# One layer of an SSD and MLP hybrid on one core: the gate's row by a transposition and DRAM instead of TensorE, and three shifts in the SSD stage's plan

## The chip, the core and the metric

The kernel runs on one core of one Trainium2 chip. The metric is the device time of one execution in microseconds (us). Three runs of the kernel before took 967.64, 968.88 and 969.93; the median, 968.88, is the time before. One further execution was taken with a profile; every duration in this text comes from it.

## The reference

One layer of a trunk with two parallel head groups. There are 256 latent tokens (`x`), 256 context tokens (`ctx`), and a width of 2048:

```
shift, scale, gate = split(silu(c) @ w_ada + b_ada, 3)            # for x; the same with c_ctx for ctx
z   = (rmsnorm(x, g_pre) * (1 + scale) + shift) @ w_in            # ctx: only the columns of x, B, C and dt
xBC = silu(depthwise_conv(z[x, B, C], width 5))                   # rows of 64 latent tokens, one row of 256 for ctx
y   = SSD forward + SSD backward                                  # 8 groups of 4 heads, chunks of 128 tokens
      # per group: CB = C B^T; y_diag = (CB * exp(min of decays)) x; states = B^T (x * decay); y_off = C states
a   = rmsnorm((y + d_skip * x) * silu(z_ssd), g_ssd)
b   = rmsnorm(u * (w_s @ rmsnorm(v, g_v) + b_s) * silu(z_mlp), g_mlp)
out = rmsnorm(concat(a, b) @ w_out, g_post)
return x + gate * out                                             # gate: one number per channel, 2048 of them
```

The scan of the latent tokens starts from the states that the context leaves, in both directions. All data is fp32. The part of the change that bears on the last line is the product `gate * g_post`, a row of 2048 numbers that must stand on all 128 partitions (called `G`), since there the tokens lie on the partitions.

## The kernel before

**Products.** Each fp32 operand is split into a rounded part (`hi`) and the rest (`lo`), and each product is three matmuls on TensorE, hi by hi, lo by hi and hi by lo (`mm3`, L139 to L143). The weights come in halves of 128 x 1024, each of which takes a cast on ScalarE (L87, L543) and a subtraction on VectorE (L88, L549) and serves 24 matmuls of the projection; the splits run some halves ahead of TensorE.

**Stages.** From 0 to about 130 us the modulation, the norm and seven channel tiles of the projection; from 130 to 445 us the SSD stage; from 445 to about 800 us the latent stage with 16 blocks for v, u and the two gate paths (`pa`, L1219 to L1221); then the out projection (L1260 to L1262) and the final norm.

**The SSD stage.** The channels of x, B and C are cut into 32 tiles of 128, ordered by group: tile 4g and 4g+1 are x of group g, 4g+2 is B, 4g+3 is C. Seven of them (0 to 3, 12, 13 and 15) are made in the first stage; 12, 13 and 15 wait in SBUF (`zq`). The loop over `REST` (L1024) makes the other 25: 48 matmuls each into a PSUM tile `psx` of the pool `acp`, which has two banks, so a tile may start once the tile before the last has been read. A C tile is needed for the latent tokens alone and has 256 columns instead of 512. After the projection a tile goes through `conv_tile` (L595): tap 0 on ScalarE (L608), eight tap instructions on VectorE (L624, the last ones that read the bank), SiLU on ScalarE (L627).

**The order of the work.** The order on TensorE, VectorE, ScalarE and GpSimd is the order in which the program issues it; only the DMA queue of SyncE (SP) is ordered by the scheduler. Between the matmuls a small planner issues the rest: `later(dt, fn)` (L578) puts a step on a list, due `dt` units from now, and `pump` (L582) moves the planner's clock on by 1.3 units after every six matmuls of a full tile (0.65 in a C tile) and issues what is due. A unit is about a microsecond. `plan_tile` (L976) gives the steps of each tile their due times. When the C tile of group g is made, it plans for that group: the scores `pcb` (L852) and the states `psc` and `psl` (L869, L872) at 6 units plus `late`; masks `cbb` and `cbf` (L860), M on GpSimd (L897); the carried states `hs`; `M` and the decayed scores in `E` (L905, L907); `pso` (L921) and its decay `yo` on VectorE (L927); the `y` sums on GpSimd (L935); the product `psy` with x (L947); its transposition `yc` (L739, called from `ssd_yc`), which goes through DRAM. For the next group it plans the four additions to the row tile R on ScalarE (`ssd_d`, L821), the minimum of the two directions into E on VectorE (`ssd_min`, L828) and the exponential of E on ScalarE (`ssd_e`, L834).

**Transposed tiles.** x and B are needed with tokens on partitions. In groups 1 to 6 they are transposed in 32 by 32 blocks on VectorE (`turn`, L738), written to DRAM and read back in four pieces by SP's queue (`turned`, L745; `bk` for B at L747, `xk` for x), with 4.5 units reserved for this (`LAND`). In groups 0 and 7 TensorE does it. `xw` and `xl` (L786, L793, GpSimd) are x times decay, the other operand of the states.

**The row load.** R of the next group, 1 MB read from one DRAM row onto all partitions, is issued on GpSimd's queue by `row_load` (L721), from `ssd_min` (L830), once E of this group no longer needs the buffer; the buffer is the only one.

**The gate.** In the latent stage VectorE multiplies each of 16 row blocks of `w_ada` by silu(c) and sums (`gate_tile`, L1070), which leaves the gate as 128 x 16 numbers, channel on the partition. After block 9 `gate_bcast` (L1075) makes G from it: g_post is read onto all partitions into G; the gate is transposed by a matmul with the identity (`psgt`, L1095), split, spread by VectorE into a block pattern (`gd`), and four matmuls with ones (`pg`, L1105) give the gate on all partitions, which VectorE multiplies into G. In the blocks nearby, `lat_t` (L1116) transposes the gated latents through DMAs on GpSimd's queue (`vt`, L1124, 16 per block), and `lat_split` (L1127) splits them, with its cast `hhi` at L1140. G is read at the end, in `o_gate` (L1311).

Of the kernel before, what the change touches and what calls it, by code (L numbers as in the profile page):

```python
# [15 lines left out]
P = 128  # L16
D = 2048
# [16 lines left out]
LAST = (-1, 4, 5, 0, 1, 2, 3, 6)  # L34

WSSD = (0, 1, 2, 3, 4, 12, 5, 6, 13, 7, 8, 14, 9, 10, 15, 11)
C_BADA, C_GPRE, C_GSSD, C_GMLP, C_BS, C_CW, C_CB, NPC = 0, 48, 64, 80, 96, 112, 272, 304


def _tile_order():  # L40
# [7 lines left out]
def tile_hybrid_ssd_mlp(  # L48
# [7 lines left out]
    pcols: bass.AP,  # L56
    dtp: bass.AP,
    dskip: bass.AP,
    gpost: bass.AP,
    gv: bass.AP,  # L60
    wst: bass.AP,
    wxbc: bass.AP,
# [66 lines left out]
    bab = stp.tile([P, KT, 2], F32, name="bab")  # L129
    nc.vector.tensor_scalar(bab[:, :, 0], pc[:, C_BADA + 16 : C_BADA + 32], 1.0, None, op0=ALU.add)  # L130
    nc.vector.tensor_copy(bab[:, :, 1], pc[:, C_BADA : C_BADA + 16])
    gate = cpool.tile([P, 48], F32, name="gate")
    nc.gpsimd.memset(gate, 0.0)
    cpool.tile([P, 64], F32, name="cpad")

# [36 lines left out]
    def spt(shape, name):  # L172
        return sps.tile(shape, F32, tag="s", name=name)
# [650 lines left out]
    def ssd_min(g, c):  # L824
        R = rows_[g]
        if c == 0:
            gs_.setdefault(g, {})["E"] = cv1.tile([P, 2, 4, P], F32, tag="E", name=f"E{g}")
        nc.vector.tensor_tensor(gs_[g]["E"][:, c], R[:, :, 0, c, :], R[:, :, 1, c, :], op=ALU.min)  # L828
        if c == 1:
            row_load(g + 1)  # L830

    def ssd_e(g):
        E = gs_[g]["E"]
# [185 lines left out]
    plan_tile(3, psx[3], 29, ds=5, late=2)  # L1019
    plan_d(17, 0, 1.3)  # L1020
    plan_e(22.5, 0)
    plan_tile(12, zq[0], 70, ds=7, tx=9)
    plan_tile(13, zq[1], 80, ds=7, tx=12.5)
    for n, i in enumerate(REST):  # L1024
        lat = ORDER[i] >= 24
# [49 lines left out]
    def gate_bcast():  # L1075
        gs.close()
        gp = ctx.enter_context(mkpool(name="gp", bufs=1, side="right"))
        G = gp.tile([P, D], F32, name="G")
        L_["G"] = G
        nc.gpsimd.dma_start(G, gpost.partition_broadcast(P))  # L1080
        nc.vector.tensor_tensor(gate[:, 0:16], gate[:, 0:16], pc[:, C_BADA + 32 : C_BADA + 48], op=ALU.add)
        nc.vector.tensor_copy(gate[:, 32:48], gate[:, 0:16])


        gh = gp.tile([48, P], F32R, name="gh")
        gl = gp.tile([48, P], F32R, name="gl")
        g1 = gp.tile([48, P], F32R, name="g1")
        gd = gp.tile([48, 4, P], F32R, name="gd")
        gk = gp.tile([48, KT], F32, name="gk")
        nc.scalar.copy(g1, ones[0:48])  # L1090
        nc.vector.tensor_tensor(gk, ident[0:48, 0:16], ident[0:48, 32:48], op=ALU.add)

        def rows():
            ps = spt([48, P], "psgt")
            nc.tensor.matmul(ps, lhsT=gate, rhs=ident, start=True, stop=True)  # L1095
            nc.scalar.copy(gh, ps)
            nc.vector.tensor_tensor(gl, ps, gh.bitcast(F32), op=ALU.subtract)
            nc.vector.tensor_copy(gh[32:48], gl[32:48].bitcast(F32))

        def expand(j):  # L1100
            nc.vector.tensor_tensor(gd, bc(gh.bitcast(F32), 1, 4), bc(gk[:, 4 * j : 4 * j + 4], 2, P), op=ALU.mult)

        def spread(j):
            p = spt([P, 512], f"pg{j}")
            nc.tensor.matmul(p, lhsT=g1, rhs=gd, start=True, stop=True)  # L1105
            gb = G[:, j * 512 : (j + 1) * 512]
            nc.vector.tensor_tensor(gb, p, gb, op=ALU.mult)
            if j < 3:
                expand(j + 1)

        later(2, rows)
        later(4, lambda: expand(0))
        for j in range(4):
            later(7 + 3 * j, lambda j=j: spread(j))
# [253 lines left out]
    man.close()  # L1368


_INS = ["xch", "xtok", "ccols", "crow", "wada", "pcols", "dtp", "dskip", "gpost", "gv", "wst", "wxbc", "wlat", "wsp", "wout"]
_OUTS = [((256, 2048), "float32")]


def _layout(i):
    import numpy as np

    i = {k: np.asarray(v) for k, v in i.items()}
    x, c, cx = i["x"][0], i["c"][0], i["ctx"][0]
    w_in, w_out, w_ada = i["w_in"][0], i["w_out"][0], i["w_ada"][0]  # L1380
    order = _tile_order()
    a = {}
    xc = np.concatenate([cx, x], axis=0)
    a["xch"] = xc.T.reshape(4, 4, P, TOK).transpose(0, 2, 1, 3).reshape(4, P, D)
    a["xtok"] = x.reshape(2, P, D)
    a["ccols"] = np.stack([c.reshape(KT, P).T, i["c_ctx"].reshape(KT, P).T], axis=2)
    wada = np.empty((48, P, D), w_ada.dtype)
    ss = w_ada[:, : 2 * D].reshape(KT, P, 2, KT, 4, 32)[:, :, ::-1].transpose(0, 1, 4, 3, 2, 5)
    sd = w_ada[KD * P :, : 2 * D].reshape((KT - KD) * P, 2, KT, P)[:, ::-1].transpose(0, 2, 1, 3)
    for kt in range(NSING):  # L1390
        r = ss[:, :, :, kt] if kt == 0 else ss[:, :, :, kt].transpose(0, 1, 3, 2, 4)
        wada[2 * kt : 2 * kt + 2] = r.reshape(2, 8, P, 256).transpose(0, 2, 1, 3).reshape(2, P, D)
    for m in range(NSING, KT, 2):
        wada[2 * m] = sd[:, m : m + 2].transpose(3, 1, 2, 0).reshape(P, D)
        wada[2 * m + 1 : 2 * m + 4] = ss[:KD, :, :, m : m + 2].reshape(3, 4, P, 512).transpose(0, 2, 1, 3).reshape(3, P, D)
    wada[32:] = w_ada[:, 2 * D :].reshape(KT, P, 16, P).transpose(2, 3, 0, 1).reshape(16, P, D)
    a["wada"] = wada
    cw = i["conv_w"][0].reshape(5, 32, P)[:, order].transpose(2, 1, 0).reshape(P, 160)
    cb = i["conv_b"][0].reshape(32, P)[order].T
    a["pcols"] = np.concatenate(  # L1400
        [i["b_ada"][0].reshape(48, P).T, i["g_pre"][0].reshape(KT, P).T, i["g_ssd"][0].reshape(KT, P).T,
         i["g_mlp"][0].reshape(KT, P).T, i["b_s"][0].T, cw, cb], axis=1)
    a["dtp"] = np.stack([i["dt_bias"][0].reshape(64), i["a_log"][0].reshape(64)])
    a["dskip"] = i["d_skip"].reshape(1, 32)
    a["gpost"] = i["g_post"].reshape(1, D)
    a["gv"] = i["g_v"].reshape(1, D)
    a["crow"] = c.reshape(1, D)
    wk = w_in.reshape(KT, P, -1)
    xbc = wk[:, :, :4096].reshape(KT, P, 32, P)[:, :, order]
    a["wst"] = np.concatenate([wk[:, :, 4096:4160], xbc[:, :, list(FIRST)].reshape(KT, P, NST * P)], axis=2)  # L1410
    a["wxbc"] = xbc[:, :, list(REST)].transpose(2, 1, 0, 3).reshape(len(REST), P, D)
    cols = {"z": 4160, "u": 6208, "v": 8256, "m": 10304}
    blocks = []
    for n in "vumz":
        w = wk[:, :, cols[n] : cols[n] + 2048].reshape(4, 4, P, 4, 512)
# [28 lines left out]
```

## Time and profile before

| what | value |
|---|---|
| median of the runs | 968.88 us |
| profiled execution, its own time | 968.23 us |
| span of its profile | 966.5 us |
| TensorE clock granted | 1.00 |
| TensorE (PE) busy | 954.9 us |
| VectorE (DVE) busy | 686.7 us |
| ScalarE (ACT) busy | 482.2 us |
| GpSimd (POOL) busy | 192.5 us |
| moved by DMA | 224.57 MB |

The span runs from the first to the last instruction that the profile shows; the execution's own time is 1.7 us longer. A row of a timeline has its start, its busy time, engine, line, operation, output<-inputs and shape; `x4` says that four instructions in a row are drawn together, and square brackets hold the idle time before it and what ended that. A row of a waiting list names the engine and instruction that waited, what it waited for, and the total, the number of times and the longest. `SPq` and `POOLq` are DMA queues. A line that groups by stretch gives the window, its sum of busy time on TensorE and then each engine's busy time with its count, the granted clock, the DMA share and GB/s.

### The profile page before, as it was taken

What the parts mean: (1) busy time and instruction counts of PE and PEld (TensorE: products, weight loads), DVE (VectorE), ACT (ScalarE), POOL (GpSimd) and SP (SyncE); (2) the same over time, 40 slices, a digit from 0 to 9 for tenths busy, and PEclk for the clock granted to TensorE, in tenths of its full rate; (3) what the DMA queues carried; (4) which work ended last, traced back from release to release, by engine and by line L of the source; (5) the groups of instructions that cost most, each with busy time, mean ns of one, the idle gap of its engine ahead of it and who ended that gap; (6) DMA issues with size and microseconds to landing.
All of it is one profiled execution on the core that took longest, in us unless ns stands there. A gap on an engine that the chain in (4) does not pass through costs nothing.

```text
span 966.5 us, 13778 instructions
## 1 busy us (share of the span) xinstructions
PE 954.9 (99%) x5142; PEld 771.1 (80%) x5142; DVE 686.7 (71%) x1116; ACT 482.2 (50%) x732; POOL 192.5 (20%) x290
## 2 busy tenths in 40 slices
PE   9999999999999999999999999999999999999997
PEld 4688888777787878787888888887888888888885
DVE  6888798879887877866667687767666665445636
ACT  4344458554555544455445333455566564346512
POOL 0000002532533414323000000043335440000000
PEclk9999999999999999999999999999999999999999
DMA  9999965566659767647877767785666666556722
GB/s 367 416 416 415 371 228 166 145 187 156 136 151 229 170 179 163 164 143 248 317 295 281 285 259 273 285 302 197 198 226 214 215 214 216 198 181 255 261 87 87
DMA packets 141490, 224.57 MB, mean 232 GB/s; under 512 B 110816, under 2 KB 111072, under 8 KB 118768
## 3 DMA queue, kind: packets, MB, share of 16 engines
q1 hardware_dynamic: 134640, 206.03, 63.2%
q0 software_dynamic: 6208, 16.85, 5.6%
q8 instruction: 40, 0.66, 0.3%
q10 hardware_dynamic: 576, 0.82, 0.2%
q14 instruction: 26, 0.21, 0.1%
HBM read 210.76 MB, written 8.72 MB: 227 GB/s over the span
## 4 chain that ended last, share of the span: by engine, by line
PE 83%; DVE 7%; DMA 5%; issue 1%; SPq 1%; POOL 1%; ACT 1%; DVEq 0%; POOLq 0%; ACTq 0%
PE pa L1219 12%; PE pa L1220 12%; PE pa L1221 12%; PE psx L141 7%; PE psx L142 6%; PE psx L143 6%; PE pm L1260 3%; PE pm L1261 3%; PE pm L1262 3%; DMA ada<-in_wada_dram 3%; DVE xbc L624 3%; PE pq L1262 2%; PE pq L1260 2%; PE pq L1261 2%; PE psada L254 2%
## 5 line engine op out<-in xcount | busy, mean ns | idle before, releaser
L88 DVE TENSOR_TENSOR lo_w<-w,hi_w 128x1024 fp32r<-128x1024 f32 x173 | 210.5, 1222 | 138.1 <-ACT hi_w L87 137.9
L87 ACT CAST hi_w<-w 128x1024 fp32r<-128x1024 f32 x173 | 181.9, 1053 | 211.1 <-PE pa L1221 139.3
L1219 PE MATMUL pa<-hi_w,hhi 128*128 128x512 f32 x512 | 201.1, 393 | 0.0
L1221 PE MATMUL pa<-hi_w,hlo 128*128 128x512 f32 x512 | 199.3, 389 | 0.0
L1220 PE MATMUL pa<-lo_w,hhi 128*128 128x512 f32 x512 | 199.3, 389 | 0.0
L141 PE MATMUL psx<-hhi,hi_w 128*128 128x512 f32 (+1 forms) x400 | 151.5, 379 | 0.2 <-DVE xbc L624 0.2
L143 PE MATMUL psx<-hhi,lo_w 128*128 128x512 f32 (+1 forms) x400 | 145.7, 364 | 0.0
L142 PE MATMUL psx<-hlo,hi_w 128*128 128x512 f32 (+1 forms) x400 | 145.6, 364 | 0.0
L1219 PEld LDWEIGHTS pa<-hi_w,hhi 128*128 128x128 f32 x512 | 96.1, 188 | 21.2 <-issue 1.6
L1221 PEld LDWEIGHTS pa<-hi_w,hlo 128*128 128x128 f32 x512 | 96.1, 188 | 20.3
L1220 PEld LDWEIGHTS pa<-lo_w,hhi 128*128 128x128 f32 x512 | 96.1, 188 | 19.5 <-issue 0.2
L624 DVE SCALAR_TENSOR_TENSOR xbc<-psx,pc,xbc 128x248 f32<-128x248 f32 (+1 forms) x204 | 83.5, 473 | 26.0 <-ACT xbc L608 25.2
L549 DVE TENSOR_TENSOR lo_w<-w,hi_w 128x1024 fp32r<-128x1024 f32 x61 | 76.8, 1265 | 19.7 <-ACT hi_w L543 19.6
L141 PEld LDWEIGHTS psx<-hhi,hi_w 128*128 128x128 f32 x400 | 75.5, 189 | 14.8 <-issue 3.5
L142 PEld LDWEIGHTS psx<-hlo,hi_w 128*128 128x128 f32 x400 | 75.5, 189 | 12.9 <-issue 1.7
L143 PEld LDWEIGHTS psx<-hhi,lo_w 128*128 128x128 f32 x400 | 75.5, 189 | 12.3
L543 ACT CAST hi_w<-w 128x1024 fp32r<-128x1024 f32 x61 | 63.5, 1044 | 29.5 <-PE psx L142 16.6
L1260 PE MATMUL pm<-hi_w,hhi 128*128 128x512 f32 x128 | 49.8, 389 | 0.0
L1261 PE MATMUL pm<-lo_w,hhi 128*128 128x512 f32 x128 | 49.8, 389 | 0.0
L1262 PE MATMUL pm<-hi_w,hlo 128*128 128x512 f32 x128 | 49.8, 389 | 0.0
L1124 POOL DMA_DIRECT2D y<-T x64 | 36.8, 583 | 47.8 <-ACT sq L1195 33.1
L1124 POOL DMA_DIRECT2D vt<-T x64 | 36.8, 584 | 47.3 <-ACT sq L1195 34.8
(277 smaller groups left out, 1424.1 us busy)
## 6 DMA issues: line engine op xcount, KB each, us to landing
w<-in_wlat_dram SPq DMA_DIRECT2D x64, 1024.0 KB, 4.9
w<-in_wout_dram SPq DMA_DIRECT2D x32, 1024.0 KB, 4.8
w<-in_wxbc_dram SPq DMA_DIRECT2D x25, 1024.0 KB, 6.0
ada<-in_wada_dram SPq DMA_DIRECT2D x24, 1024.0 KB, 13.9
gate<-in_wada_dram SPq DMA_DIRECT2D x16, 1024.0 KB, 5.0
ada<-in_wada_dram SPq DMA_DIRECT2D x16, 512.0 KB, 12.4
R<-acs POOLq DMA_DIRECT2D x8, 1024.0 KB, 7.1
wst<-in_wst_dram SPq DMA_DIRECT2D x15, 480.0 KB, 13.0
```

The source lines that it names most:

```text
L87: nc.scalar.copy(hi, raw)
L88: nc.vector.tensor_tensor(lo, raw, hi.bitcast(F32), op=ALU.subtract)
L141: nc.tensor.matmul(ps, lhsT=whi, rhs=hhi[k][:, s], start=start, stop=False)
L142: nc.tensor.matmul(ps, lhsT=whi, rhs=hlo[k][:, s], start=False, stop=False)
L143: nc.tensor.matmul(ps, lhsT=wlo, rhs=hhi[k][:, s], start=False, stop=stop)
L624: nc.vector.scalar_tensor_tensor(ao, zi, cw[:, k : k + 1], ao, op0=ALU.mult, op1=ALU.add)
L1219: nc.tensor.matmul(pa[tk], lhsT=hhi[k][:, t], rhs=whi[:, w], start=k == 0, stop=False)
L1220: nc.tensor.matmul(pa[tk], lhsT=hhi[k][:, t], rhs=wlo[:, w], start=False, stop=False)
L1221: nc.tensor.matmul(pa[tk], lhsT=hlo[k][:, t], rhs=whi[:, w], start=False, stop=k == KT - 1)
L1260: nc.tensor.matmul(p, lhsT=yh[:, t], rhs=whi[:, w], start=j == 0, stop=False)
L1261: nc.tensor.matmul(p, lhsT=yh[:, t], rhs=wlo[:, w], start=False, stop=False)
L1262: nc.tensor.matmul(p, lhsT=yl[:, t], rhs=whi[:, w], start=False, stop=hf == 0 and j == 15)
```

## The change

**Gate's row.** g_post is no input of its own any more; it comes as 16 more columns of the table `pcols` (`C_GPOST`), channel on the partition like the gate. `gate_bcast` adds the bias and multiplies by g_post on VectorE (128 x 16), transposes the 128 x 32 tile in blocks of 32 on VectorE, writes the row to DRAM with four DMAs and reads it onto all partitions with one, all five on GpSimd's queue, right after block 9. The matmuls `psgt` and `pg`, their casts and their tiles are gone. Since one argument line is gone, a line such as L852 before is L851 after, up to this function.

**SSD: three numbers.** `late`, the delay of all steps of a group after its C tile, grows by 3 units where B goes through DRAM (groups 1 to 6): 11 becomes 14, and 14 becomes 17 in group 3. The row load of group 5 is issued 12 units after its minimum instead of at once. And tile 12, the first x tile of group 3 that waits in SBUF, is planned from 63 instead of 70.

```diff
-C_BADA, C_GPRE, C_GSSD, C_GMLP, C_BS, C_CW, C_CB, NPC = 0, 48, 64, 80, 96, 112, 272, 304
+C_BADA, C_GPRE, C_GSSD, C_GMLP, C_BS, C_CW, C_CB, C_GPOST, NPC = 0, 48, 64, 80, 96, 112, 272, 304, 320
...
-    gate = cpool.tile([P, 48], F32, name="gate")
+    gate = cpool.tile([P, 32], F32, name="gate")
...
         if c == 1:
-            row_load(g + 1)
+            later(12 if g == 4 else 0, lambda: row_load(g + 1))
...
         if lb == LAND:
-            late = max(late, 14.0 if i == 15 else 11.0)
+            late = max(late, 17.0 if i == 15 else 14.0)
...
-    plan_tile(12, zq[0], 70, ds=7, tx=9)
+    plan_tile(12, zq[0], 63, ds=7, tx=9)
...
-        nc.gpsimd.dma_start(G, gpost.partition_broadcast(P))
         nc.vector.tensor_tensor(gate[:, 0:16], gate[:, 0:16], pc[:, C_BADA + 32 : C_BADA + 48], op=ALU.add)
-        nc.vector.tensor_copy(gate[:, 32:48], gate[:, 0:16])
-        gh = gp.tile([48, P], F32R, name="gh")
-        gl = gp.tile([48, P], F32R, name="gl")
-        g1 = gp.tile([48, P], F32R, name="g1")
-        gd = gp.tile([48, 4, P], F32R, name="gd")
-        gk = gp.tile([48, KT], F32, name="gk")
...
-        def rows():
-            ps = spt([48, P], "psgt")
-            nc.tensor.matmul(ps, lhsT=gate, rhs=ident, start=True, stop=True)
...
-        def spread(j):
-            p = spt([P, 512], f"pg{j}")
-            nc.tensor.matmul(p, lhsT=g1, rhs=gd, start=True, stop=True)
-            gb = G[:, j * 512 : (j + 1) * 512]
-            nc.vector.tensor_tensor(gb, p, gb, op=ALU.mult)
...
+        nc.vector.tensor_tensor(gate[:, 0:16], gate[:, 0:16], pc[:, C_GPOST : C_GPOST + 16], op=ALU.mult)
+        gt = gp.tile([P, 32], F32, name="gt")
+        nc.vector.transpose(gt, gate)
+        row = drp.tile([16, P], F32, name="grow")
+        for a in range(4):
+            nc.gpsimd.dma_start(row[:, 32 * a : 32 * a + 32], gt[32 * a : 32 * a + 16])
+        nc.gpsimd.dma_start(G, row.rearrange("j p -> (j p)").unsqueeze(0).partition_broadcast(P))
...
```

What this does to the order of the instructions is shown at two places. Names carry the tile or group and a running number (`psx16` is the projection of tile 16, `psc2` belongs to group 2), and `x2` says that two alike stand together.

First, the products of group 2 on TensorE, with the projection of tile 16 around them, before:

```order
L143 MATMUL psx16_2496<-hhi11_127,lo_w19_2415 128x512
L852 MATMUL pcb2_2559<-xbc11_2401,xbc10_2312 128x128 x2
L869 MATMUL psc2_2562<-xw2_2428,bk2_2417 128x512 x2
L872 MATMUL psl2_2565<-xl2_2460,bk2_2417 128x256 x2
L141 MATMUL psx16_2496<-hhi12_128,hi_w19_2403 128x512
```

and after the change:

```order
L142 MATMUL psx16_2499<-hhi15_131,lo_w19_2416 128x512
L851 MATMUL pcb2_2586<-xbc11_2402,xbc10_2318 128x128 x2
L868 MATMUL psc2_2589<-xw2_2434,bk2_2418 128x512 x2
L871 MATMUL psl2_2592<-xl2_2464,bk2_2418 128x256 x2
L140 MATMUL psx17_2595<-hhi0_116,hi_w20_2458 128x512
```

The three products have moved from ahead of the last twelve matmuls of tile 16 to the end of that tile; the next tile's first matmul stands behind them.

Second, VectorE between the last decayed scores of group 1 (`E1`) and the taps of tile 10, which free that tile's bank, before:

```order
L907 TENSOR_TENSOR E1_2079<-M11_2208,E1_2079 128x512
L927 TENSOR_TENSOR yo10_2235<-pso10_2210,ed_1460 128x512
L927 TENSOR_TENSOR yo11_2241<-pso11_2211,ed_1460 128x512
L549 TENSOR_TENSOR lo_w16_2277<-w8_1975,hi_w16_2254 128x1024
L739 STREAM_TRANSPOSE tx21_2279<-xbc9_2180 128x4x4x32
L739 STREAM_TRANSPOSE yc1_2283<-psy1_2262 128x4x4x32
L828 TENSOR_TENSOR E2_2287<-R2_2090 128x512 x2
L624 SCALAR_TENSOR_TENSOR xbc10_2312<-psx10_2173,pc_87,xbc10_2312 128x4x62
```

and after the change:

```order
L906 TENSOR_TENSOR E1_2079<-M11_2220,E1_2079 128x512
L548 TENSOR_TENSOR lo_w16_2254<-w8_1975,hi_w16_2235 128x1024
L623 SCALAR_TENSOR_TENSOR xbc12_2246<-y_68,pc_87,xbc12_2246 128x4x62
...
L738 STREAM_TRANSPOSE tx21_2264<-xbc9_2163 128x4x4x32
L926 TENSOR_TENSOR yo10_2268<-pso10_2229,ed_1460 128x512
L926 TENSOR_TENSOR yo11_2274<-pso11_2230,ed_1460 128x512
L738 STREAM_TRANSPOSE yc1_2305<-psy1_2296 128x4x4x32
L827 TENSOR_TENSOR E2_2309<-R2_2090 128x512 x2
L623 SCALAR_TENSOR_TENSOR xbc10_2318<-psx10_2156,pc_87,xbc10_2318 128x4x62
```

The eight taps of tile 12 (the first of them is shown) now stand ahead of `yo`, of `yc` and of the taps of tile 10; before, they stood behind the latter. On ScalarE tap 0 of tile 10 stands ahead of the exponential of E of group 2, where it stood behind it:

```order
L543 CAST hi_w16_2254<-w8_1975 128x1024
L821 ACTIVATE R2_2090<-R2_2090,y_68 128x128 x4
L834 ACT_TABLE_LOAD
L834 ACTIVATE E2_2287<-E2_2287 128x1024
L608 ACTIVATE xbc10_2312<-psx10_2173,pc_87 128x512
```

```order
L820 ACTIVATE R2_2090<-R2_2090,y_68 128x128 x8
L607 ACTIVATE xbc10_2318<-psx10_2156,pc_87 128x512
L542 CAST hi_w17_2320<-w8_1975 128x1024
L833 ACT_TABLE_LOAD
L833 ACTIVATE E2_2309<-E2_2309 128x1024
```

The first piece is ScalarE before, the second ScalarE after: the table load and the exponential have moved behind tap 0 and a weight cast.

On GpSimd the load of R for group 5 (`R5`) stood behind the two `y` sums of group 3 and ahead of `xw4`; after the change it stands behind `xw4`, both sums, `xl4` and the skip product of group 4:

```order
L934 TENSOR_TENSOR y_68<-y_68,yo30_2991 128x256 x2
L785 TENSOR_TENSOR xw4_3007<-xk4_2698,ed_1460 128x256 x4
L934 TENSOR_TENSOR y_68<-y_68,yo31_3003 128x256 x2
L792 TENSOR_TENSOR xl4_3055<-xk4_2698,ed_1460 128x256 x2
L913 TENSOR_TENSOR y_68<-xk4_2698,dsk_108 128x256 x2
L724 DMA R5_3155<-acs_1461 128x2048
```

That is GpSimd after the change; the load now comes last of the six.

More of the change, by code (lines that the diff above doesn't have):

```diff
@@ L58, in tile_hybrid_ssd_mlp @@
     dskip: bass.AP,
-    gpost: bass.AP,
     gv: bass.AP,
@@ L1079, in gate_bcast @@
         L_["G"] = G
-        nc.gpsimd.dma_start(G, gpost.partition_broadcast(P))
         nc.vector.tensor_tensor(gate[:, 0:16], gate[:, 0:16], pc[:, C_BADA + 32 : C_BADA + 48], op=ALU.add)
-        nc.vector.tensor_copy(gate[:, 32:48], gate[:, 0:16])
-        gh = gp.tile([48, P], F32R, name="gh")
-        gl = gp.tile([48, P], F32R, name="gl")
-        g1 = gp.tile([48, P], F32R, name="g1")
-        gd = gp.tile([48, 4, P], F32R, name="gd")
-        gk = gp.tile([48, KT], F32, name="gk")
-        nc.scalar.copy(g1, ones[0:48])
-        nc.vector.tensor_tensor(gk, ident[0:48, 0:16], ident[0:48, 32:48], op=ALU.add)
-        def rows():
-            ps = spt([48, P], "psgt")
[L1095 to L1101, printed above, removed]
-        def spread(j):
-            p = spt([P, 512], f"pg{j}")
-            nc.tensor.matmul(p, lhsT=g1, rhs=gd, start=True, stop=True)
-            gb = G[:, j * 512 : (j + 1) * 512]
-            nc.vector.tensor_tensor(gb, p, gb, op=ALU.mult)
[L1108 to L1114, printed above, removed]
+        nc.vector.tensor_tensor(gate[:, 0:16], gate[:, 0:16], pc[:, C_GPOST : C_GPOST + 16], op=ALU.mult)
[5 more added lines that the diff above has]
+        nc.gpsimd.dma_start(G, row.rearrange("j p -> (j p)").unsqueeze(0).partition_broadcast(P))
     def lat_t(kind, j4):
@@ L1368, in tile_hybrid_ssd_mlp @@
     man.close()
-_INS = ["xch", "xtok", "ccols", "crow", "wada", "pcols", "dtp", "dskip", "gpost", "gv", "wst", "wxbc", "wlat", "wsp", "wout"]
+_INS = ["xch", "xtok", "ccols", "crow", "wada", "pcols", "dtp", "dskip", "gv", "wst", "wxbc", "wlat", "wsp", "wout"]
 _OUTS = [((256, 2048), "float32")]
@@ L1401, in _layout @@
         [i["b_ada"][0].reshape(48, P).T, i["g_pre"][0].reshape(KT, P).T, i["g_ssd"][0].reshape(KT, P).T,
-         i["g_mlp"][0].reshape(KT, P).T, i["b_s"][0].T, cw, cb], axis=1)
+         i["g_mlp"][0].reshape(KT, P).T, i["b_s"][0].T, cw, cb, i["g_post"].reshape(KT, P).T], axis=1)
     a["dtp"] = np.stack([i["dt_bias"][0].reshape(64), i["a_log"][0].reshape(64)])
     a["dskip"] = i["d_skip"].reshape(1, 32)
-    a["gpost"] = i["g_post"].reshape(1, D)
     a["gv"] = i["g_v"].reshape(1, D)
```

## The prediction

> **What bounds the kernel now.** I read the page first, then busy time by stretch, then the waits of TensorE alone, and last the timeline of every place that the change touches.
>
> ```profile
> span 966.5 us, 13778 instructions
> PE 954.9 (99%) x5142; PEld 771.1 (80%) x5142; DVE 686.7 (71%) x1116; ACT 482.2 (50%) x732; POOL 192.5 (20%) x290
> ...
> 445.00:930.00 485.00, 485.00 (x2168) 400.65 (x2167) 310.85 (x367) 247.56 (x321) 79.09 (x139) 1.00 0.70 247
> ```
>
> TensorE is busy for 954.9 of 966.5 us, and from 445 to 930 us it has no gap at all (485.00 of 485.00). So a microsecond taken off its stream there is a microsecond off the end, and work on the other engines costs nothing until TensorE waits for it. The second list is short: these are its waits in the SSD stage (130 to 445 us).
>
> ```profile
> PE psc L869 <- DMA bk<-Db: 2.8, 2, 1.4
> ...
> PE psx L141 <- DVE xbc L624: 0.2, 1, 0.2
> ```
>
> Columns: total us, times, longest. Twice it waits for a transposed B tile that comes back from DRAM, and once, briefly, for a PSUM bank. So the change has two things to win, TensorE instructions and the waits on `bk`, and one thing to lose: the wait on the bank.
>
> **Gate's row.** The change removes from TensorE one product `psgt` and four `pg`. What each costs is read from the starts of the projection's matmuls around it, since matmuls overlap.
>
> ```profile
> 656.09 0.39 PE L1219 MATMUL pa<-hi_w,hhi 128*128 128x512 f32 x1
> ...
> 656.54 0.39 PE L1221 MATMUL pa<-hi_w,hlo 128*128 128x512 f32 x1
> 656.86 0.42 PE L1095 MATMUL psgt<-ident,gate 128*48 128x128 f32 x2
> ...
> 657.78 0.39 PE L1221 MATMUL pa<-hi_w,hlo 128*128 128x512 f32 x1
> ...
> 662.56 0.39 PE L1221 MATMUL pa<-hi_w,hlo 128*128 128x512 f32 x1
> ...
> 663.88 0.40 PE L1221 MATMUL pa<-hi_w,hlo 128*128 128x512 f32 x1
> ```
>
> From 656.09 to 656.54 are two steps, so a step is 0.225 us. Three steps after 656.54 would be 657.22; the third matmul starts at 657.78, so `psgt` costs 0.56. Around the first `pg`, three steps after 662.56 would be 663.24; it is 663.88, so 0.64. One `psgt` and four `pg`: 0.56 + 4 x 0.64 = **3.1 us**, all on the path. Their vector and scalar companions go too and were never waited for.
>
> What is added is one small product, one 32-column transposition on VectorE and five DMAs on GpSimd's queue, the last of which (G) waits for the four before it to land. Behind it in that queue stand the transfers of `vt`.
>
> ```profile
> 635.36 4.63 POOL L1124 DMA_DIRECT2D vt<-T x8 [5.90 <-ACT hi_w L87]
> ...
> 654.51 1.70 ACT L1140 ACTIVATE hhi<-vt,gc 128x256 fp32r<-128x256 f32 x4
> ...
> 939.75 0.69 DVE L1311 TENSOR_TENSOR og<-ob,G 128x512 f32<-128x512 f32 x1
> ```
>
> G itself is wanted at 939.75, 300 us later: nothing. The `vt` transfers start at 635.36 and are read at 654.51. The queue is idle for 5.9 us before them; I estimate that the five DMAs take that and up to 3 us more. If ScalarE then waits 3 us, the weight casts behind it are late by 3 us; they run up to four halves of twelve matmuls (4 x 2.7 us) ahead of TensorE. Cost 0; without that cover, 3 us.
>
> **The products with B, later.** In groups 1 to 6 `pcb`, `psc` and `psl` stand 3 planner units later, which puts them at the end of a projection tile. Group 3 had no wait and is the measure for the two that had.
>
> ```profile
> 238.69 0.60 PE L852 MATMUL pcb<-xbc,xbc 128*128 128x128 f32 x4
> 240.72 1.96 PE L869 MATMUL psc<-xw,bk 128*128 128x512 f32 x4 [1.42 <-DMA bk<-Db]
> ...
> 268.16 0.60 PE L852 MATMUL pcb<-xbc,xbc 128*128 128x128 f32 x4
> 268.61 1.88 PE L869 MATMUL psc<-xw,bk 128*128 128x512 f32 x4
> ...
> 301.70 0.60 PE L852 MATMUL pcb<-xbc,xbc 128*128 128x128 f32 x4
> 303.66 1.52 PE L869 MATMUL psc<-xw,bk 128*128 128x512 f32 x3 [1.35 <-DMA bk<-Db]
> ```
>
> From `pcb` to `psc`: 0.45 in group 3, 2.03 in group 2, 1.96 in group 4. The excess is 1.58 + 1.51 = **3.1 us**. Both products move past twelve matmuls of the same tile (12 x 0.225 = 2.7 us), more than either excess, so both waits go if `bk` comes no later than now. In group 4 something else helps:
>
> ```profile
> 291.86 0.59 POOL L725 DMA_DIRECT2D R<-acs x1 [2.09 <-DVE E L828]
> 292.46 2.33 POOL L786 TENSOR_TENSOR xw<-xk,ed 128x256 f32<-128x256 f32 x4
> ...
> 292.90 6.00 SPq L747 DMA_DIRECT2D bk<-Db x4
> ...
> R<-acs POOLq DMA_DIRECT2D x1, 1024.0 KB, 10.7
> ```
>
> The megabyte of R for group 5 starts 1 us before the four pieces of `bk`, whose issue then takes 6.00 us. In the new order R stands behind `xw`, half of the `y` sums, `xl` and the skip product of group 4 on GpSimd, and the transposition of B stands ahead of the `y` sum and the two `yo` on VectorE: `bk` earlier, R later. R later by 2.33 + 1.2 + 1.2 + about 2 = 7 us is asked for at 298.6 and lands at 309.3 at the latest. ScalarE first adds to it after it has copied group 4's product, which ends after 305.2 today. It could wait some 4 us; behind it then stand a SiLU and a weight cast that TensorE needs two tiles later. Cost 0; without that cover, 4 us.
>
> **Where it can lose: the bank.** The score products `psy` of a group move with the rest, from the middle of a tile to its end. In groups 1, 4, 5 and 6 the next tile is a C tile of 256 columns, half as long, and the tile after it needs the bank of the tile just ended. Today's place of that wait, in group 1:
>
> ```profile
> 219.53 0.47 PE L141 MATMUL psx<-hhi,hi_w 128*128 128x512 f32 x1 [0.22 <-DVE xbc L624]
> ...
> 206.88 0.69 DVE L907 TENSOR_TENSOR E<-M,E 128x512 f32<-128x512 f32 x1
> 207.49 1.28 DVE L927 TENSOR_TENSOR yo<-pso,ed 128x512 f32<-128x512 f32 x2
> 208.69 1.38 DVE L549 TENSOR_TENSOR lo_w<-w,hi_w 128x1024 fp32r<-128x1024 f32 x1
> 209.99 0.70 DVE L739 STREAM_TRANSPOSE tx<-xbc 128x512 f32<-128x512 f32 x1
> 210.62 0.67 DVE L739 STREAM_TRANSPOSE yc<-psy 128x512 f32<-128x512 f32 x1
> 211.22 1.84 DVE L828 TENSOR_TENSOR E<-R 128x512 f32<-128x512 f32 x2
> 216.19 3.19 DVE L624 SCALAR_TENSOR_TENSOR xbc<-psx,pc,xbc 128x248 f32<-128x248 f32 x8 [3.13 <-ACT xbc L608]
> ...
> 213.14 1.28 ACT L834 ACT_TABLE_LOAD   x1 [4.22 <-DVE E L828]
> ...
> 215.40 0.76 ACT L608 ACTIVATE xbc<-psx,pc 128x512 f32<-128x512 f32 x1
> ```
>
> Today the taps of tile 10 begin at 216.19 because ScalarE makes the exponential of E (table at 213.14) before tap 0 (215.40), and VectorE is idle for 3.13 us. In the new order tap 0 stands ahead of the table, so that idle goes. In its place stand the taps of tile 12, seven units sooner. Their price depends on what runs beside them:
>
> ```profile
> 220.19 3.04 POOL L786 TENSOR_TENSOR xw<-xk,ed 128x256 f32<-128x256 f32 x4 [6.25 <-DMA xk<-Dx]
> ...
> 220.44 6.08 DVE L624 SCALAR_TENSOR_TENSOR xbc<-y,pc,xbc 128x248 f32<-128x248 f32 x8
> ...
> 232.95 3.22 DVE L624 SCALAR_TENSOR_TENSOR xbc<-y,pc,xbc 128x248 f32<-128x248 f32 x8
> ```
>
> The same eight taps with both inputs in SBUF take 6.08 beside `xw` on GpSimd and 3.22 with GpSimd idle. In the new place GpSimd's next instruction is the `y` sum, which waits for a `yo` that stands behind these taps on VectorE, so I take 3.2. Chain: the last product of E ends where it does now, at 207.6 (the later product fills time in which VectorE waited); then weight rest 1.2, taps 3.2, `tx` 0.6, two `yo` 1.3, so `yc` starts at 213.9, then `yc` 0.6, E 1.84, taps of tile 10 3.19 and 0.15 to release: 219.7. TensorE is ready at 219.53 - 0.22 = 219.3 in both. A wait of 0.4 in place of 0.22: **+0.2**.
>
> In groups 4 to 6 nothing is ahead of `yc`:
>
> ```profile
> 317.74 1.09 PE L947 MATMUL psy<-E,xk 128*64 128x128 f32 x16
> ...
> 322.98 0.28 PE L141 MATMUL psx<-hhi,hi_w 128*128 128x256 f32 x1
> ...
> 328.73 0.40 PE L141 MATMUL psx<-hhi,hi_w 128*128 128x512 f32 x1
> ```
>
> From the start of `psy`, TensorE takes about 1.0 for it, 0.15 to change over and 5.75 for the C tile: 6.9. VectorE takes 1.09 + 0.05 + 0.6 + 1.84 + 3.19 + 0.15 = 6.9. That is no margin, and no loss either: **+0.1** for all three, up to 0.5 each.
>
> **The sum.** -3.1 - 3.1 + 0.2 + 0.1 = -5.9 us against the profiled execution's own 968.23 (its span is 966.5): 962.3. The median of the runs shown is 968.88, 0.65 above it; with the same -5.9 it is **963.0**. A difference under 0.2% (1.9 us) can hardly be told from none.
>
> **Rivals.**
> 1. *Tile 12's taps meet GpSimd.* They then take 6.1 and not 3.2, `psy`'s chain in group 1 ends 2.9 us later, and the time is 965.9. For it: the 6.08 row. Against it: GpSimd's place in the order. [...] Chance 0.13.
> 2. *The waits on `bk` stay.* The order of SP's queue changes too: `bk` of group 2 now stands behind a weight load and `xk`. If both waits move along, 3.1 comes back: 966.1; if one does, 964.5. Against it: B is transposed sooner in both groups. Chance 0.10.
> 3. *Slower.* The chain through `yc`, E and the taps no longer fits under the C tile in groups 1, 4, 5 and 6. It would have to be 2.0 us too long in each to eat the 6.2 won and 1.9 more, and at 2.5 each the time is 968.9 - 6.2 + 10 = 972.7. For it: the margin is nil by my rows. Against it: every instruction of the chain is counted at its dearest. Chance 0.05.
> 4. *Nothing to measure.* Waits of 1 to 1.5 in each of the four, or 3 us where `vt` is late and more at the bank, leave 967 to 969. Chance 0.06.
>
> The forecast itself, both gains with up to 1.5 us of new waiting, has 0.66. Its lower end is every gain and the bank's 0.22 too, 968.88 - 6.2 - 0.22 = 962.5, less 1.1 us, about half of what the runs shown span (2.3): 961.4. The upper end takes in rivals 1 and 2 in full, 966.3. Faster by over 0.2% are the forecast, nearly all of rivals 1 and 2 (those with more waiting besides fall short): 0.86. Within 0.2%: 0.09. Slower: 0.05.
>
> **What would show it.** Right: no `psgt` and `pg`; no wait of `psc` on `bk` in the list; a wait of TensorE on the taps of tile 10 below 1 us and at most a few tenths at the tiles after the C tiles of groups 4 to 6; taps of tile 12 in about 3.2 us; no gap from 445 to 930. Wrong: `psx` waiting on taps for several us (rivals 1 and 3, told apart by the group), `psc` waiting on `bk` (rival 2), or a gap after 640 us where `vt` is split.

## The result, and the profile after

The changed kernel takes **962.13 us** (median of six runs, 961.99 to 962.90) against 968.4 for the kernel before (six runs, 967.56 to 969.93): a ratio of 0.9935 with a 95% interval of 0.9923 to 0.9948. The forecast was 963.0, with a range of 961.4 to 966.3. The profiled execution takes 962.26; that of before took 968.23, so 6.0 us went. The score products `psy` of the last group start 2.85 sooner than before (438.38 against 441.23), and 3.1 more went after it; the stage itself began 0.2 later than in the profile of before, so it gained 3.05.

The page's head, and then the busy time of the stretch from 445 to 930 us, of the new kernel:

```profile
span 960.5 us, 13751 instructions
PE 951.7 (99%) x5136; PEld 770.5 (80%) x5136; DVE 675.3 (70%) x1106; ACT 482.4 (50%) x730; POOL 190.5 (20%) x294
```

```profile
445.00:930.00 485.00, 485.00 (x2173) 402.75 (x2172) 303.33 (x355) 245.34 (x315) 78.84 (x138) 1.00 0.69 245
```

TensorE is still busy in every microsecond of that stretch: the end came forward only because six matmuls fewer stand in it (one product with the identity that was drawn as two, and four more) and because it begins 2.85 us sooner. All of TensorE's waits of 0.2 us and more, in total, times and longest:

```profile
PE px L1334 <- ACT dg L1333: 1.5, 1, 1.5
PE psw L322 <- DVE ones L110: 1.1, 1, 1.1
PE psx L140 <- DVE xbc L623: 0.4, 1, 0.4
PE pss L344 <- ACT y L340: 0.3, 1, 0.3
PE psada L253 <- DMA ada<-in_wada_dram: 0.3, 1, 0.3
PE psada L224 <- DMA ada<-in_wada_dram: 0.2, 1, 0.2
```

The 2.8 us on `bk` are gone, and the wait at the bank has grown from 0.22 to 0.39. The products with B, in groups 2 and 4 of the new kernel:

```profile
241.77 0.60 PE L851 MATMUL pcb<-xbc,xbc 128*128 128x128 f32 x4
242.21 1.88 PE L868 MATMUL psc<-xw,bk 128*128 128x512 f32 x4
...
303.16 0.60 PE L851 MATMUL pcb<-xbc,xbc 128*128 128x128 f32 x4
303.60 1.88 PE L868 MATMUL psc<-xw,bk 128*128 128x512 f32 x4
...
232.14 2.26 SPq L746 DMA_DIRECT2D bk<-Db x4
...
288.47 4.92 SPq L746 DMA_DIRECT2D bk<-Db x4
```

From `pcb` to `psc` it is 0.44 in both, against 0.45 in group 3 before; the 2.03 and 1.96 are gone. The last two rows are the reading of `bk` in the two groups. It starts at 288.47 in group 4, against 292.90 before, and at 232.14 in group 2, against 234.46 before. So two things changed for these waits: the products stand later, and `bk` comes sooner. VectorE in group 1, from the last product of E to the taps of tile 10, and the GpSimd sum beside it:

```profile
207.17 0.69 DVE L906 TENSOR_TENSOR E<-M,E 128x512 f32<-128x512 f32 x1
207.78 1.22 DVE L548 TENSOR_TENSOR lo_w<-w,hi_w 128x1024 fp32r<-128x1024 f32 x1
208.91 3.22 DVE L623 SCALAR_TENSOR_TENSOR xbc<-y,pc,xbc 128x248 f32<-128x248 f32 x8
212.05 0.71 DVE L738 STREAM_TRANSPOSE tx<-xbc 128x512 f32<-128x512 f32 x1
212.68 1.25 DVE L926 TENSOR_TENSOR yo<-pso,ed 128x512 f32<-128x512 f32 x2
213.85 0.70 DVE L738 STREAM_TRANSPOSE yc<-psy 128x512 f32<-128x512 f32 x1
214.47 2.19 DVE L827 TENSOR_TENSOR E<-R 128x512 f32<-128x512 f32 x2
216.58 3.18 DVE L623 SCALAR_TENSOR_TENSOR xbc<-psx,pc,xbc 128x248 f32<-128x248 f32 x8
...
213.41 3.84 POOL L934 TENSOR_TENSOR y<-y,yo 128x256 f32<-128x256 f32 x4 [7.45 <-DVE yo L926]
```

The row at 208.91 is the taps of tile 12: 3.22 us, with GpSimd idle until 213.41. Every link of the chain that the prediction wrote out is here, in its order, and `yc` starts at 213.85 (forecast 213.9). Group 4, the first of the three groups without a margin by the prediction:

```profile
318.94 1.09 PE L946 MATMUL psy<-E,xk 128*64 128x128 f32 x16
...
325.81 0.40 PE L140 MATMUL psx<-hhi,hi_w 128*128 128x512 f32 x1
...
320.08 0.72 DVE L738 STREAM_TRANSPOSE yc<-psy 128x512 f32<-128x512 f32 x1 [2.23 <-PE psy L946]
320.72 1.25 DVE L827 TENSOR_TENSOR E<-R 128x512 f32<-128x512 f32 x2
321.89 3.19 DVE L623 SCALAR_TENSOR_TENSOR xbc<-psx,pc,xbc 128x248 f32<-128x248 f32 x8
```

The taps end at 325.08, TensorE goes on at 325.81 without a wait: some 0.7 us to spare.

### The profile page after: what moved, and what is told of

It reads as the page before. It is cut to its first block, busy times and chain, and to the rows that moved or that the text cites. A ratio compares the mean times of both kernels' runs of the same rounds, so it can differ in the third digit from the quotient of the medians.

```text
span 960.5 us, 13751 instructions
## 1 busy us (share of the span) xinstructions
PE 951.7 (99%) x5136; PEld 770.5 (80%) x5136; DVE 675.3 (70%) x1106; ACT 482.4 (50%) x730; POOL 190.5 (20%) x294
## 4 chain that ended last, share of the span: by engine, by line
PE 92%; DMA 4%; DVE 2%; ACT 0%; issue 0%; SPq 0%; POOL 0%; ACTq 0%; POOLq 0%
PE pa L1191 12%; PE pa L1193 12%; PE pa L1192 12%; PE psx L140 9%; PE psx L141 9%; PE psx L142 9%; PE pm L1234 3%; PE pm L1232 3%; PE pm L1233 3%; DMA ada<-in_wada_dram 3%; PE pq L1234 2%; PE pq L1233 2%; PE pq L1232 2%; PE psada L253 2%; PE psc L868 1%; PE pso L920 1%
## 5 line engine op out<-in xcount | busy, mean ns | idle before, releaser
L1071 DVE SCALAR_TENSOR_TENSOR junk<-gate,cb 128x2048 bf16<-128x2048 f32 x16 | 36.6, 2290 | 13.2 <-DMA gate<-in_wada_dram 13.2
```

## The experiments

Times are medians against runs of the kernel before on the same chip (968.5 to 968.9 there). Two theories stood at the start. One: the gain is TensorE's own work in the gate (3.1) and the products with B standing later (3.1), and the bank is the one place where it is given back. The other: tile 12's shift or R's later load do part of it.

**The gate alone.** The three numbers of the SSD stage as before.

```diff
-            later(12 if g == 4 else 0, lambda: row_load(g + 1))
+            row_load(g + 1)
-            late = max(late, 17.0 if i == 15 else 14.0)
+            late = max(late, 14.0 if i == 15 else 11.0)
-    plan_tile(12, zq[0], 63, ds=7, tx=9)
+    plan_tile(12, zq[0], 70, ds=7, tx=9)
```

> The gate's row by VectorE and DRAM, with the SSD numbers of the kernel before (11/14, the row load at once, tile 12 at 70). Theory (the gate is worth its TensorE steps, 3.1 us, and the SSD numbers the rest): 968.4 - 3.1 = 965.3, with both waits of psc on bk (1.4 us each) still in the list and no gap of TensorE from 445 to 930 us. Rival (the five DMAs and G's landing hold vt up): over 966.5, with a gap after 640 us.

Measured: 965.65 (964.57 to 967.72), ratio 0.9967 (0.9954 to 0.9980): 3.0 us less than before, as expected (1.9 to 4.5 by the interval). The profiled execution was the slowest of the five, 967.72, and shows something that the expectation did not have. Group 4 waits longer here, and the clock drops behind the wait:

```profile
301.24 0.60 PE L851 MATMUL pcb<-xbc,xbc 128*128 128x128 f32 x4
304.51 2.86 PE L868 MATMUL psc<-xw,bk 128*128 128x512 f32 x4 [2.67 <-DMA bk<-Db]
```

```profile
305.00:306.00 1.00, 1.00 (x3) 0.53 (x2) 0.71 (x3) 0.00 (x0) 0.54 (x1) 0.71 0.94 136
306.00:307.00 1.00, 1.00 (x2) 0.34 (x1) 0.28 (x1) 0.00 (x0) 0.50 (x1) 0.50 0.93 122
...
308.00:309.00 1.00, 1.00 (x4) 0.82 (x3) 0.00 (x0) 0.00 (x0) 0.93 (x2) 0.58 1.04 344
```

The third number from the right is the granted clock; it is 0.50 between the rows shown. It is halved from 305.42 (0.71 is 0.42 us at full and 0.58 at half) to 308.84, 3.4 us, which costs 1.7 us of TensorE's work on top of the 2.67 of waiting.

**Late back at 11.** The new kernel, with only `late` undone.

```diff
-            late = max(late, 17.0 if i == 15 else 14.0)
+            late = max(late, 14.0 if i == 15 else 11.0)
```

> The new kernel with late back at 11 and 14; tile 12 stays at 63 and the row load of group 5 stays late. Theory: the products with B then stand twelve matmuls sooner and group 2's psc waits for bk again, 1.5 us; group 4's may not, since R no longer collides; and on VectorE the taps of tile 12 stand right behind yo, so that the y sum on GpSimd runs beside them: about 6 us instead of 3.2 and some 3 us of wait at the bank in group 1. Together 962.1 + 4.5 = 966.6, more (968) if group 4 waits too. Rival (the wait for bk had gone because B is transposed sooner, not because the products stand later): no wait of psc, 962 to 963.

Measured: 968.46, ratio 0.9995 (0.9986 to 1.0004): the time is that of before again. New waiting eats all that the gate's row wins. The wait is at the bank, 3.8 us in one piece with a halved clock behind it (0.83 from 223.5 to 224.0 us, 0.50 to 227.0, 0.76 to 227.5: 3.4 us at half), and `psc` waits only 0.3, since its data had time to arrive meanwhile. VectorE in group 1, of this kernel:

```profile
207.35 1.28 DVE L926 TENSOR_TENSOR yo<-pso,ed 128x512 f32<-128x512 f32 x2
208.55 1.38 DVE L548 TENSOR_TENSOR lo_w<-w,hi_w 128x1024 fp32r<-128x1024 f32 x1
209.94 4.59 DVE L623 SCALAR_TENSOR_TENSOR xbc<-y,pc,xbc 128x248 f32<-128x248 f32 x8
...
220.05 3.19 DVE L623 SCALAR_TENSOR_TENSOR xbc<-psx,pc,xbc 128x248 f32<-128x248 f32 x8 [3.13 <-ACT xbc L607]
```

Here the `y` sum on GpSimd starts at 208.12 and tile 12's taps take 4.59 instead of 3.22: the first rival of the prediction does happen when `yo` stands ahead of the taps. It is worth 1.4, not 2.9; the rest of the delay is the 3.13 of idle before the taps of tile 10, because tap 0 stands behind the exponential on ScalarE again. The expectation had the place right and the total 1.9 us too small: it took the taps for the delay, and left out this idle and the clock. What it was made for, to tell whether the waits on `bk` went because the products stand later or because B is transposed sooner, it can't tell, since the wait at the bank holds the products up here.

**Tile 12 back at 70.** The new kernel with 70 for 63.

> The new kernel with tile 12 planned from 70 as before. The taps of tile 10 then have no taps of tile 12 ahead of them. Theory: the wait at the bank in group 1 (0.4) goes, nothing else moves: 961.7, so tile 12's shift gains nothing beside late 14. Rival: the x of group 3 comes too late, and psc of group 3 waits 1 us or more: 963 or above.

Measured: **961.37** (961.23 to 961.98), ratio 0.9922 (0.9910 to 0.9935), no wait at the bank in TensorE's list and no wait of `psc`. The shift of tile 12 costs 0.4 us of waiting and gains nothing here.

**R's load alone, and R's load at once.** First the gate's row with R's load 12 units later and the other two numbers as before; then the new kernel with the load at once.

```diff
-            late = max(late, 17.0 if i == 15 else 14.0)
+            late = max(late, 14.0 if i == 15 else 11.0)
-    plan_tile(12, zq[0], 63, ds=7, tx=9)
+    plan_tile(12, zq[0], 70, ds=7, tx=9)
```

> The gate's row as in the new kernel, and of the SSD numbers only the row load of group 5 at 12 units later (late 11/14, tile 12 at 70). Theory (group 4's wait of psc for bk is R's megabyte beside the four pieces of bk): that wait, 2.7 us in the profile of the kernel with the gate alone, goes or falls below 0.5, group 2's 1.2 stays; with the slow clock behind a wait of 2.7 gone too, 963 to 964. Rival (group 4's B is transposed too late, R has no part in it): both waits stay, 965.6.

```diff
-            later(12 if g == 4 else 0, lambda: row_load(g + 1))
+            row_load(g + 1)
```

> The new kernel with the row load of group 5 issued at once. Theory (with late 14 the products with B of group 4 stand 3 us or more behind the landing of bk, so that R may collide): no wait of psc, 961.9 to 962.4. Rival (R's delay is needed beside late 14 too): psc of group 4 waits 1 us or more, 963.1 or above, over 965 if the wait passes 2 us and the slow clock follows it.

Measured: 965.44 (ratio 0.9969, 0.9957 to 0.9980) and 962.24 (0.9932, 0.9920 to 0.9944). TensorE's waits in the timeline of the first:

```profile
240.69 1.95 PE L868 MATMUL psc<-xw,bk 128*128 128x512 f32 x4 [1.84 <-DMA bk<-Db]
...
303.52 1.96 PE L868 MATMUL psc<-xw,bk 128*128 128x512 f32 x4 [1.20 <-DMA bk<-Db]
```

Both waits stay, and the time is that of the gate alone (965.65), as the rival of the expectation had it. But R's megabyte was not out of the way of group 4's `bk` in this run:

```profile
293.04 2.08 SPq L746 DMA_DIRECT2D bk<-Db  x4
294.60 0.59 POOL L724 DMA_DIRECT2D R<-acs  x1
...
DMA to landing us min/median/max: 5.4/6.8/8.8
```

R was issued only 2.7 us later than before (294.60 against 291.86), together with the last of the four pieces. The last row is the time from issue to landing of these pieces: the first two, well ahead of R, took 5.4 and 5.5 us, the last one 8.8, and it landed at 303.38, right behind R (303.23). Before, with R ahead of all four, they landed from 302.91 to 303.53, again right behind R (302.56). So the trace rather speaks for R holding `bk` up in group 4. An estimate from these rows: with 5.5 us the last piece would have landed at 300.1, ahead of the products, which were due at 302.2 (0.44 behind `pcb`). No run kept R away from `bk` at late 11, so this stays open. Group 2, with no R beside it, waits all the same. With late 14, R's load at once makes no difference: it is issued at 293.64, behind all four pieces, since these start at 288.26.

**Late 14 alone beside the gate.** Tile 12 at 70 and R's load at once, both undone.

> The gate's row and late 14/17 as in the new kernel, but tile 12 at 70 and the row load of group 5 at once, as before. Theory (of the three numbers of the SSD stage only late is worth time): no wait of psc, no wait at the bank, 961.4 like the kernel with tile 12 at 70 alone. Rival (one of the other two is needed once both are undone): psc of group 4 or 3 waits 1 us or more, 962.5 or above.

Measured: 961.52 (961.44 to 961.68), ratio 0.9922 (0.9908 to 0.9935); no wait of `psc`, none at the bank. Of the three numbers, `late` does all the work.

**The bank's margin.** The minimum into E once more in the groups whose chain runs under a C tile.

```diff
+        if c == 1 and g in (2, 5, 6, 7):
+            for q in range(2):
+                nc.vector.tensor_tensor(gs_[g]["E"][:, q], R[:, :, 0, q, :], R[:, :, 1, q, :], op=ALU.min)
```

> The new kernel with the minimum into E computed twice in groups 2, 5, 6 and 7 (the same data, two more instructions, 1.25 us between yc and the taps that free the bank). Theory by the trace of the new kernel: the taps end 0.8, 0.8 and 0.2 us before TensorE needs the bank in groups 4, 5 and 6, and 0.4 after it in group 1; with about 0.1 for the release the waits are 1.65, 0.55, 0.55 and 1.15, so 3.4 us more: 965.5. By the prediction's nil margin in groups 4 to 6: 1.25 in each of the four, 967.1. Rival (the bank does not bind there, another wait covers it): within 0.5 of 962.1.

Measured: 968.91 (967.38 to 970.82), ratio 0.9997 (0.9987 to 1.0007). The waits:

```profile
PE psx L140 <- DVE xbc L623: 3.0, 3, 2.1
PE pa L1194 <- DVE xbc L623: 1.9, 1, 1.9
```

In groups 4 and 5 they are 0.45 each (`pa` is the first tile behind group 6's C tile), near the 0.55 of the theory: the addition made the taps start 1.2 later, so the margin is about 0.75 there. In groups 1 and 6 they are 2.14 and 1.87, since the added minimum takes 1.82 and 2.12 beside GpSimd's work instead of 1.25. That makes 4.5 us more of waiting instead of the 3.4 expected, and in the profiled run a halved clock behind the 2.14 (0.76 from 222.5 to 223.0 us, 0.50 to 226.0, 0.83 to 226.5: 3.4 us at half). The runs lie between 967.38 and 970.82; four of the eleven, at 967.4 to 967.5, have a mean clock of 0.998, the others 0.995 to 0.997. The expectation of 965.5 was 3.4 too low. Rival 3 of the prediction can happen: 1.2 to 2.0 us more in this chain in four groups cost all that the change gained.

**The clock behind a wait.** To see it by itself, only E of group 5 is computed 3, 4 and 5 times (the loop runs over 4, 6 and 8 added instructions), so that one wait grows and nothing else does.

```diff
+        if c == 1 and g == 5:
+            for q in range(4):
+                nc.vector.tensor_tensor(gs_[g]["E"][:, q % 2], R[:, :, 0, q % 2, :], R[:, :, 1, q % 2, :], op=ALU.min)
```

> The new kernel with the minimum into E of group 5 computed three times instead of once (the same data, four more instructions of 0.63 us, 2.5 us), so that TensorE waits for the bank once, after group 4, and nowhere else for longer than before. By the margin of 0.7 us that the first lengthening showed there, the wait is 1.8 us. Theory (a wait of TensorE of more than about 2 us is followed by some 3.4 us at half clock, which costs 1.7 more): no slow clock here, 962.1 + 1.8 = 963.9, perhaps in some runs 965.6. Rival (the slow clock has nothing to do with waits): 963.9, clock full in all three lengths.

> The same with the minimum computed four times (3.75 us more): a wait of 3.05 us. Theory: the clock is halved behind the wait for about 3.4 us, so 962.1 + 3.05 + 1.7 = 966.9. Rival: 965.2.

> The same with the minimum computed five times (5.0 us more): a wait of 4.3 us. Theory: halved once behind it, 962.1 + 4.3 + 1.7 = 968.1, or more if a longer wait keeps the clock down for longer. Rival: 966.4.

Measured: 964.09, 966.56 and 968.89. The wait in the three profiles:

```profile
327.63 0.47 PE L140 MATMUL psx<-hhi,hi_w 128*128 128x512 f32 x1 [1.66 <-DVE xbc L623]
```

```profile
328.90 0.47 PE L140 MATMUL psx<-hhi,hi_w 128*128 128x512 f32 x1 [2.86 <-DVE xbc L623]
```

```profile
329.95 0.76 PE L140 MATMUL psx<-hhi,hi_w 128*128 128x512 f32 x1 [4.07 <-DVE xbc L623]
```

With 1.66 of waiting all five runs lie between 964.05 and 964.13. With 2.86 the ten runs fall into two heaps: three at 965.02 to 965.28, with a mean clock of 0.999 over the execution, and seven at 966.47 to 967.12, with 0.996 or 0.997. The lower heap is the wait alone (962.13 + 2.86 = 965.0), the upper one 1.5 to 2.1 us more than that. The profiled run of the upper heap, by microseconds:

```profile
329.00:330.00 1.00, 1.00 (x4) 0.86 (x5) 1.00 (x2) 0.98 (x2) 0.83 (x1) 0.83 0.95 352
330.00:331.00 1.00, 1.00 (x4) 0.71 (x4) 1.00 (x1) 0.99 (x3) 1.00 (x1) 0.50 0.95 380
...
332.00:333.00 1.00, 1.00 (x4) 0.81 (x3) 0.93 (x3) 0.35 (x1) 1.00 (x3) 0.50 0.02 3
333.00:334.00 1.00, 1.00 (x5) 0.76 (x5) 1.00 (x2) 0.42 (x1) 1.00 (x3) 0.96 0.00 0
```

Half clock from 329.66 to 333.08, again 3.4 us. With 4.07 of waiting the eleven runs again lie in two heaps: five at 967.72 to 968.22, with a mean clock of 0.996 or 0.997, and six at 968.89 to 969.52, with 0.994 or 0.995. None is at the 966.2 of the wait alone. The profiled run (969.25) is of the upper heap:

```profile
328.00:329.00 1.00, 0.00 (x0) 0.00 (x0) 1.00 (x4) 0.99 (x2) 0.00 (x0) 0.71 1.40 250
329.00:330.00 1.00, 0.05 (x1) 0.08 (x1) 1.00 (x4) 1.00 (x2) 0.67 (x2) 0.50 0.75 270
...
335.00:336.00 1.00, 1.00 (x5) 0.76 (x5) 1.00 (x2) 0.02 (x1) 1.00 (x1) 0.88 0.00 0
```

The clock is halved from 328.42, while TensorE still waits, to 335.24: 6.8 us, twice 3.4. The lower heap lies 1.5 to 2.0 above the wait alone, as one stretch of 3.4 would have it; no profile caught a run of it.

**More transfers ahead of `vt`.** G is broadcast four times.

```diff
         nc.gpsimd.dma_start(G, row.rearrange("j p -> (j p)").unsqueeze(0).partition_broadcast(P))
+        nc.gpsimd.dma_start(G, row.rearrange("j p -> (j p)").unsqueeze(0).partition_broadcast(P))
+        nc.gpsimd.dma_start(G, row.rearrange("j p -> (j p)").unsqueeze(0).partition_broadcast(P))
+        nc.gpsimd.dma_start(G, row.rearrange("j p -> (j p)").unsqueeze(0).partition_broadcast(P))
```

> The new kernel with the broadcast of G from DRAM issued four times instead of once (the same data). GpSimd's queue then holds three more transfers of a megabyte ahead of vt, each some 8 us to landing. Theory (the weight casts of ScalarE run four halves of 2.7 us ahead of TensorE, so vt may be late by about 10 us): if the three go one after the other, vt is 20 us or more late and TensorE has a gap after 660 us of 5 to 15 us; if they overlap and vt is less than 10 us late, no gap and 962.1. Rival (vt has no such cover, every microsecond is paid): the gap is as long as vt's delay.

Measured: 962.29 (0.9932, 0.9920 to 0.9944), no gap. But the added loads were spread between the `vt` transfers of three blocks (G is issued at 634.95, 650.50, 663.22 and 671.75), and `vt` made ScalarE wait 1.2 us only. So the cover was not used up, and how far it reaches stays open.

**A version that beats both.** With tile 12 at 70, the second x tile of group 7 goes through VectorE and DRAM as well, in place of four TensorE transpositions; group 7's steps stand one unit later.

```diff
-        return g == 0 or g == NGRP - 1 and what != "x0"
+        return g == 0 or g == NGRP - 1 and what not in ("x0", "x1")
...
-            d0 += late
+            d0 += 1 if i == 31 else late
```

> The new kernel with tile 12 at 70 (no wait at the bank), and the second x tile of group 7 transposed on VectorE through DRAM instead of by four TensorE transpositions, with group 7's steps one unit later so that xl is ready. Theory (each such step off TensorE is worth what it takes there, about 0.6 us as psgt did): 961.4 - 0.6 = 960.8. Rival (xk lands too late, or GpSimd's xw does): psc of group 7 waits, above 961.4.

Measured: **960.75** (960.45 to 961.66), ratio 0.9919 (0.9907 to 0.9931). All five runs are below the fastest of the changed kernel (961.99). Against the kernel with tile 12 at 70 alone the median is 0.6 less, as expected, but the runs of the two overlap (961.23 to 961.98 there) and so do the intervals. TensorE is busy for 1.0 us less (951.5 there):

```profile
span 958.7 us, 13755 instructions
PE 950.5 (99%) x5132; PEld 770.1 (80%) x5132; DVE 675.8 (70%) x1107; ACT 482.3 (50%) x729; POOL 193.0 (20%) x294
```

## Why the prediction was right, point by point

- **The gate, 3.1 us.** Right: 3.1 between the two profiles behind the SSD stage, and 3.0 between the medians where it was changed alone. In the profile of the gate alone it is 3.1 too: the SSD stage ends 2.56 later than before there, by the longer waits, and the end comes 0.54 sooner. The cover held: `vt` is split at 651.72, 2.8 sooner than before (654.51), like everything around it. G took 8.2 us to land, and GpSimd waited for it in the middle of the `vt` transfers:

```profile
634.68 4.07 POOL L1096 DMA_DIRECT2D vt<-T x7 [0.31 <-issue]
642.31 4.61 POOL L1096 DMA_DIRECT2D vt<-T x8 [3.56 <-DMA G<-grow]
...
651.72 1.70 ACT L1112 ACTIVATE hhi<-vt,gc 128x256 fp32r<-128x256 f32 x4
```

- **The waits on `bk`, 3.1 us.** Right: both are gone, and the stage gained 3.05. Late 14 alone does it; late 11 with R's load moved keeps both. The prediction's ground was that the products stand later, if `bk` comes no later than it did. In fact `bk` came sooner, as the prediction also said: in group 2 its last piece landed at 238.25 against 240.59, in group 4 at 296.36 against 303.53. Both follow from `late`: with late 14 alone beside the gate, `bk` lands at 237.57 and 295.48. In group 4, `yo` now stands behind the transposition of B on VectorE, where it stood ahead of it. By these times either the later products or the sooner `bk` would have been enough; no run takes them apart. That R's megabyte holds up `bk` in group 4 carried no number in the prediction, and was not tested cleanly. R was issued at 296.19, 4.3 later than before and not 7, and landed at 302.3; ScalarE's first addition to it starts at 306.0, so its later load costs nothing.
- **The bank, +0.2.** The wait is 0.39 for the 0.4, but the closeness is in part luck. The minimum into E took 2.19 and not 1.84, with the `y` sum beside it, so the chain ended 0.2 later than forecast. TensorE was ready 0.2 later too (219.52 and not 219.3), since the whole stage began 0.2 later than in the profile of before. That tile 12's taps stand in this chain is the whole of the wait: with tile 12 at 70 there is none.
- **Groups 4 to 6, +0.1.** Too dear by a little: no wait at all. The prediction took 1.84 for the minimum in each; it is 1.25 in groups 4 and 5 and 1.85 in group 6, so that the margin is some 0.7, 0.7 and 0.1.
- **The median.** 962.13 for 963.0. Of the 0.9, less than 0.1 is the sum itself (962.26 profiled for 962.3). The rest is chance of the draw: the median of before, from three runs, lies above its profiled execution by 0.65, and that of the new kernel below its own by 0.13. With the six runs of before (968.4) the same sum gives 962.5. The new kernel's runs span 0.9 us, those of before beside the experiments 967.6 to 971.3; the ones of before above 970.2 show a mean clock of 0.996 to 0.998. The likely reason is that the wait on `bk`, 1.42 and 1.35 in the profile of before, is longer in some executions and has the half clock behind it, as the 2.67 has in the profile of the gate alone; no profile of the kernel before caught such an execution, so that is argued, not shown.
- **The rivals.** 1 (GpSimd beside tile 12's taps) and 3 (the chain too long) did not happen, though both did in the experiments: with late at 11 the taps took 4.59 beside the `y` sum, and with the longer chain the bank's waits were 0.45 to 2.14. 2 (`bk` waits stay) did not happen. In rivals 1 and 3 the prediction priced a wait at its length; behind waits of 2.14 us and more in one piece the profiles of the experiments show 3.4 us at half clock, so both could have cost some 1.7 more each time.

## What to carry to other kernels

Where TensorE has no gaps, as here from 445 to 930 us, a transposition or a broadcast of a row is worth moving to another engine and DRAM for what each such step takes there (some 0.6 us for each of the gate's five products, 3.0 between the medians), if its result is wanted late. A wait can be removed by putting the waiting instruction later in its own stream; look then at what else moves with it, since here the data came sooner too. After that, ask of each other number that was moved with it what it does alone: here two of three did nothing or cost something. And ask of an experiment's trace whether its edit did what it was meant to do, since the planner's 12 units moved R by 2.7 us. A wait is not priced by its length alone: from 2.14 us on, stretches at half clock (3.4 and 6.8 us in the profiles) followed in many executions of this kernel, and the times scattered.

## What the runs showed of the hardware that was not expected

In the SSD stage the granted clock stayed at 1.00 behind waits of TensorE of 1.35 and 1.42 us (the profile of before), 1.66 (group 5's minimum three times), 1.84 (R's load alone) and 1.87 (the longer chain). Behind waits of 2.14 (the longer chain), 2.67 (the gate alone), 2.86 (the minimum four times) and 3.80 us (late at 11) it fell to half for about 3.4 us in the profiles, 1.7 us of TensorE's work, and with 4.07 (the minimum five times) for 6.8 us, from within the wait on. It does not happen in every execution: by the times and mean clocks, with 2.86 it did in seven of ten runs and not in the other three.

Two kinds of instructions on VectorE took longer in these runs with GpSimd at work beside them, by very different amounts: the eight taps of tile 12 took 3.22 alone (the new kernel) and 4.59 beside the `y` sum (late at 11), and the minimum into E took 1.25 alone (groups 4 and 5 of the new kernel) and 1.82 to 2.19 with GpSimd at work for all or part of it (groups 1 and 6 of the new kernel and of the longer chain).
